# Gathering the second down product one set later, its row split moved up to the rows' multiplication

## The chip, the cores and the metric

The kernel runs on one core of one Trainium2 chip. The metric is the device time of one execution in microseconds (us); lower is better. The engines are named as the profile names them: PE (TensorE matmuls), PEld (its weight loads), DVE (VectorE), ACT (ScalarE), POOL (GpSimd) and SP (SyncE, which here only issues DMA transfers).

## What is computed

Two transformer layers over 512 tokens of width 1024: a gated mixing layer, then an attention layer with a forget gate, each followed by a feed-forward block. The change touches only the feed-forward block, which both layers run:

```python
h = h + rmsnorm(mixed @ w_out[layer], ln_mix_post[layer])
f = rmsnorm(h, ln_ffn_pre[layer])
f = (jax.nn.silu(f @ w_ffn_gate[layer]) * (f @ w_ffn_up[layer])) @ w_ffn_down[layer]
h = h + rmsnorm(f, ln_ffn_post[layer])
```

All of it is float32. `D_FF` is 2816, that is 22 blocks of 128 hidden rows.

## The kernel before

**Precision.** A float32 operand is split into two parts: `hi`, a cast to the PE's float32 format on ACT (L267), and `lo`, the rest, a subtraction on DVE (L268). `mm3` (L208 to L212) multiplies hi by hi, one hi by the other's lo, and lo by hi: three matmuls for each product of two tiles. Weights are split as `whi` and `wlo` (eight buffers each), the rows of a down product as `ff`.

**Sets.** Sixteen of the 22 hidden blocks go through a seven-product scheme in place of eight products. `Seven` (L1028) computes one *set*: two blocks of gate or of up. Its products are numbered 1 to 7 and run in the order 1, 7, 6, 4, 2, 5, 3; product 3 is run after products 1 and 7 of the next set. A product is twelve matmuls 256 wide and needs one weight split (512 wide). `form` makes the weight sums on DVE (L1055, L1056, L1059, L1061). For a gate set from j = 2 on, two sums come ready from DRAM; an up set makes all four, beginning with L1055, which reads both halves of a freshly loaded pair of weight tiles. Those tiles (`raw`) have four buffers; a new load waits until the last weight split of the tile that had the buffer is done. The loop over j = 0 to 7 (`ones` is 8) alternates a gate set and an up set; I call the two a *pair*. At the end of a set its rows come out: L1095 adds the two PSUM results and so frees their bank; `gate_rows` (L1224) multiplies by the norm and applies Silu; `up_rows` (L1230) multiplies the up rows by the gate rows: row 1 first (L1232, into `room`, called `u1`), then row 0 (L1234, into `u0`). `Down.sums` (L1110) then makes the sums that the down products need.

**Down products.** The result of pair j goes into a `Down` object, which also has seven products, here P0 to P6, each six matmuls 512 wide: three for each of two token blocks. Each needs the split of 256 columns of its rows (`ff`, six buffers of tag `p`, shared with other tiles) and a weight split. P2 accumulates over all j into one pair of PSUM banks, `kept` (tag `tr`, two buffers; the trace names the tiles `x`), while the gate and up sets go on; `straight` (L1246) loads its weights `a12`, runs it and makes `last_sum`. The other products run afterwards: a first pass over j with P0, P3, P5, P6, then a second pass with P1 and P4. I write P2(j), P5(j) and so on for those of pair j.

**Where P2 stands before.** In the loop of L1253 the condition L1272 calls `straight(j - 1, False)` after the up set for j = 1 and after the gate set for every later j. The last one, P2(7), stands in the first pass between P3(0) and P5(0); after it two ACT copies (L1306) empty `kept`, and its two banks are given to P6, which accumulates over j.

**Order.** The program's text gives a priority; a scheduler then fixes one order of instructions for each engine and of DMA issues on SP. In the trace every engine but the weight loads goes through its rows in that order, so an instruction that waits holds up those behind it. The matmul order on PE stays close to the text; DVE, ACT and SP are interleaved by the scheduler.

Of the kernel before, what the change touches and what calls it, by code (L numbers as in the profile page):

```python
# [8 lines left out]
F32R = mybir.dt.float32r  # L9
# [6 lines left out]
P = 128  # L16
# [19 lines left out]
HALVES = ((0, 256), (256, 512))  # L36
# [6 lines left out]
def hybrid(ctx: ExitStack, tc: tile.TileContext, i: dict, out: bass.AP):  # L43
# [4 lines left out]
    tp = ctx.enter_context(tc.tile_pool(name="temps", bufs=4))  # L48
# [9 lines left out]
    def name(s):  # L58
        n_of[s] = n_of.get(s, 0) + 1
        return f"{s}_{n_of[s]}"  # L60
# [4 lines left out]
    def plain(s, shape=(P, T), dt=F32):  # L65
        return yp.tile(list(shape), dt, tag="y", name=name(s))
# [4 lines left out]
    def temp(s, shape=(P, T), tag="t", bufs=4, dt=F32):  # L71
        return tp.tile(list(shape), dt, tag=tag, name=name(s), bufs=bufs)
# [12 lines left out]
    o = ps("tr", s="idle")  # L85
# [122 lines left out]
    def mm3(o, w, x, start, stop, more=False):  # L208

        PE.matmul(o, w[0], x[0], start=start, stop=False, skip_group_check=more)  # L210
        PE.matmul(o, w[0], x[1], start=False, stop=False, skip_group_check=more)  # L211
        return PE.matmul(o, w[1], x[0], start=False, stop=stop, skip_group_check=more)  # L212
# [53 lines left out]
    def split(src, hi, lo, eng=None):  # L266
        last_hi[0] = A.copy(hi, src)  # L267
        last_split[0] = last_hi[0], (eng or V).tensor_sub(lo, src, hi)  # L268
# [14 lines left out]
    class Norm:  # L283


        def __init__(self, width=T):
            self.r4 = small("r4")
            self.acc, self.width = None, width
# [739 lines left out]
    class Seven:  # L1028
# [20 lines left out]
        def form(self, n):  # L1049

            a11, a12, a21, a22 = self.a11, self.a12, self.a21, self.a22
            if n == 7:
                if not self.summed:
                    self.s3 = temp("s3")
                    V.tensor_add(self.s3, a11, a21)  # L1055
                    V.tensor_add(a21, a21, a22)  # L1056
                return self.s3
            if n == 6:
                V.tensor_add(a11, a21, a11)  # L1059
            elif n == 3:  # L1060
                V.tensor_add(a12, a11, a12)  # L1061
            return {1: a11, 2: a12, 3: a12, 4: a22, 5: a21, 6: a11}[n]

        def product(self, o, x, n, more=False):
            pair = pair_of_parts()
            split(self.form(n), *pair)
            for k, w in enumerate(cut(pair, P)):
                mm3(o, w, self.xs[x][k], k == 0 and not more, k == KT // 2 - 1, more)
# [33 lines left out]
    class Down:  # L1102
# [2 lines left out]

        def __init__(self, layer, k, u0, u1, t):
            self.layer, self.k, self.u0, self.u1, self.t = layer, k, u0, u1, t
            self.forms = {}

        def sums(self):  # L1110

# [33 lines left out]

        def product(self, n, o, start, stop):

            left, right = (slice(*c) for c in HALVES)
            if n == 3:
                V.tensor_add(self.a11, self.a21, self.a11)  # L1150
            elif n == 5:
                V.tensor_add(self.a12, self.a11, self.a12)
            src = {0: "a11", 1: "s3", 2: "a12", 3: "a11", 4: "a22", 5: "a12", 6: "a21"}[n]
            u, c = {0: (self.u0, left), 1: (self.t, left), 2: (self.u1, left), 3: (self.t, right),
                    4: (self.u1, left), 5: (self.u1, right), 6: (self.u0, right)}[n]
            both = tp.tile([P, 2, 256], F32R, tag="p", name=name("ff"), bufs=6)
            split(u[:, c], both[:, 0], both[:, 1])
            w = pair_of_parts()
            split(getattr(self, src), *(x.rearrange("p (m c) -> p m c", c=P) for x in w))
            for t in range(2):  # L1160
                tokens = slice(t * P, (t + 1) * P)
                mm3(o[t], (both[:, 0, tokens], both[:, 1, tokens]), w, start, stop, True)

    def feed_forward(layer, phase, xp, meanwhile=None):
# [3 lines left out]
        ones = 8  # L1168
# [47 lines left out]
        downs, gates = [], {}  # L1216
# [13 lines left out]
        def up_rows(row, u, some):  # L1230
            if row:
                V.scalar_tensor_tensor(out=u, in0=u, scalar=-1.0, in1=gates[1], op0=ALU.mult, op1=ALU.mult)  # L1232
            else:
                V.tensor_mul(u, u, gates[0])  # L1234
            if some:
                split(u, *some[row])
            elif not row:
                downs[-1].sums()

        def sets(m, some=None):  # L1240
            sums_ahead()
            yield Seven(xs, "w_gate", layer, m, "mm", gate_rows)
            sums_ahead()
            yield Seven(xs, "w_up", layer, m, "lg", lambda row, u: up_rows(row, u, some), None if some else places)

        def straight(j, last):  # L1246
            d = downs[j]
            d.weights(0)
            d.product(2, kept, False, last)
            d.last_sum()  # L1250

        before = lambda: None
        for j in range(ones):  # L1253
            if j == 0:
                us = list(sets(2))
                for n in (1, 2):
                    for u in us:
                        u.run(n)
                for n in (7, 6, 4, 5):
                    for u in us:  # L1260
                        u.run(n)
                us[0].run(3)
                before = us[1]
                continue
            for n, u in enumerate(sets(2 + 2 * j)):
                u.run(1)
                u.run(7)
                before.run(3)
                for x in (6, 4, 2, 5):
                    u.run(x)  # L1270
                before = u
                if n == (j == 1):  # L1272
                    straight(j - 1, False)
        before.run(3)

        o = {0: [ps("mm", s="p") for _ in range(2)], 3: [ps("lg", s="p") for _ in range(2)]}
        one, two = [act("ua", F32) for _ in range(2)], [act("ub", F32) for _ in range(2)]

        def tap(n):

            for t in range(2):
                x, y = o[n][t], ys[t]
                z = ys[2 + t]
                if n == 0:
                    A.copy(one[t], x)
                    V.tensor_add(y[0], x, y[0])
                elif n == 3:
                    V.tensor_add(one[t], x, one[t])
                elif n == 6:
                    V.tensor_add(two[t], x, one[t])  # L1290
                elif n == 5:
                    V.tensor_add(z[0], x, z[0])
                elif n == 1:
                    V.tensor_add(z[1], x, z[1])
                    V.tensor_add(y[1], x, y[1])
                else:
                    V.tensor_add(y[1], x, y[1])

        for j, d in enumerate(downs):
            d.weights(1)  # L1300
            for n in (0, 3, 5, 6) if j == 0 else (0, 3, 6, 5):
                if j == 0 and n == 5:
                    straight(ones - 1, True)
                    for t in range(2):
                        ys[t][0] = plain("y")
                        A.copy(ys[t][0], kept[t])  # L1306
                    o[5] = [ps(tag, s="p") for tag in ("mm", "lg")]
                    o[6] = [ps("tr", s="p") for _ in range(2)]
                d.product(n, o[n], j == 0, j == ones - 1)
                if j == ones - 1:  # L1310
                    tap(n)
        o.update({1: [ps("mm", s="q") for _ in range(2)], 4: [ps("lg", s="q") for _ in range(2)]})
        late = [(z, t, d) for z, d, some in ((2, 0, two), (2, 1, two), (0, 1, one)) for t in range(2)]
        for j, d in enumerate(downs):
# [5 lines left out]
            if j < len(late):  # L1320
                z, t, dh = late[j]
                y = ys[z + t][dh]
# [350 lines left out]
```

## Time and profile before

| | |
|---|---|
| median of 3 runs | 1110.28 us (1109.08 to 1110.86) |
| the profiled execution | 1109.39 us, its span 1107.7 us |
| PE busy | 1087.1 us, 98% of the span |
| PEld | 985.4 us, 89% |
| DVE | 934.4 us, 84% |
| ACT | 733.0 us, 66% |
| POOL | 59.7 us, 5% |

The profiled execution took 0.89 us less than the median. A row of the timeline gives start, duration, engine, source line, operation, `out<-in`, and in brackets how long the engine had stood idle and what ended the wait. Matmul durations overlap, since they are pipelined: what a matmul costs in a stream is the distance to the next start. The windows view gives busy time by engine in a stretch, then the granted share of the PE clock, the DMA engines' busy share and GB/s.

The loop over the pairs lies at about 200 to 378 us in the first layer and 784 to 964 us in the second.

### The profile page before, as it was taken

The numbers are of one execution on the slowest core, as the hardware profiler recorded it, in microseconds if no ns is written. First come the engines' busy times: TensorE is split into PE (matmuls) and PEld (weight loads), VectorE is DVE, ScalarE is ACT, GpSimd is POOL, SyncE is SP. The second block draws the span as 40 slices with busy tenths as digits, with TensorE's granted clock in tenths as the row PEclk, the third lists the DMA queues.
The fourth block names the chain that finished last, engine by engine and source line by source line (L and its number), as shares of the span: only waits on it lengthen the run. The fifth ranks groups of instructions, "written<-read, shape, count | busy, mean of one in ns | idle before, by whom it ended". The sixth has DMA issues, their size and how long they took to land.

```text
span 1107.7 us, 19986 instructions
## 1 busy us (share of the span) xinstructions
PE 1087.1 (98%) x7286; PEld 985.4 (89%) x7286; DVE 934.4 (84%) x1839; ACT 733.0 (66%) x1609; POOL 59.7 (5%) x74
## 2 busy tenths in 40 slices
PE   9999999999999999999999999999999999999997
PEld 7998889999999888998988898889999899888996
DVE  7889658988887999986987798858998887999975
ACT  8776468665666667677666677768666566666563
POOL 0100001001100000000000000011011010000000
PEclk9999999999999999999999999999999999999999
DMA  7522346498788445563322654445499779444622
GB/s 268 160 79 77 96 114 202 113 248 210 213 209 206 142 139 168 207 183 104 103 90 62 175 130 113 138 114 177 127 244 223 211 195 223 142 127 136 216 78 77
DMA packets 126378, 172.69 MB, mean 156 GB/s; under 512 B 7820, under 2 KB 91800, under 8 KB 126280
## 3 DMA queue, kind: packets, MB, share of 16 engines
q1 hardware_dynamic: 114920, 153.93, 45.2%
q0 software_dynamic: 10944, 17.30, 10.0%
q8 instruction: 57, 0.93, 0.3%
q14 instruction: 41, 0.34, 0.1%
q10 hardware_dynamic: 416, 0.18, 0.1%
HBM read 155.04 MB, written 39.85 MB: 176 GB/s over the span
## 4 chain that ended last, share of the span: by engine, by line
PE 79%; DVE 10%; ACT 3%; DMA 3%; issue 3%; SPq 1%; POOL 0%; DVEq 0%; POOLq 0%; ACTq 0%
PE a L210 5%; PE a L211 5%; PE a L212 5%; DVE wlo L268 5%; PE y L210 4%; PE y L211 4%; PE y L212 4%; PE ps L212 3%; PE ps L211 3%; PE ps L210 3%; PE p L212 3%; PE p L210 3%; PE p L211 3%; PE e L210 2%; PE e L211 2%
## 5 line engine op out<-in xcount | busy, mean ns | idle before, releaser
L267 ACT CAST whi<-raw 128x512 fp32r<-128x512 f32 x476 | 286.0, 619 | 122.6 <-PE a L211 21.7
L268 DVE TENSOR_TENSOR wlo<-raw,whi 128x512 fp32r<-128x512 f32 x476 | 316.7, 684 | 39.1 <-ACT whi L267 34.8
L210 PE MATMUL a<-xshi,whi 128*128 128x256 f32 x480 | 136.7, 285 | 0.0
L211 PE MATMUL a<-xslo,whi 128*128 128x256 f32 x480 | 136.2, 284 | 0.0
L212 PE MATMUL a<-xshi,wlo 128*128 128x256 f32 x480 | 135.9, 283 | 0.0
L210 PEld LDWEIGHTS a<-xshi,whi 128*128 128x128 f32 x480 | 91.8, 191 | 1.7 <-ACT e L1094 0.6
L211 PEld LDWEIGHTS a<-xslo,whi 128*128 128x128 f32 x480 | 91.9, 191 | 0.8
L212 PEld LDWEIGHTS a<-xshi,wlo 128*128 128x128 f32 x480 | 91.8, 191 | 0.0
L211 PE MATMUL ps<-xslo,whi 128*128 128x256 f32 x192 | 53.9, 283 | 0.6 <-DVE xslo L268 0.6
L212 PE MATMUL ps<-xshi,wlo 128*128 128x256 f32 x192 | 54.3, 285 | 0.0
L210 PE MATMUL ps<-xshi,whi 128*128 128x256 f32 x192 | 53.7, 287 | 0.0
L210 PE MATMUL y<-whi,mixedhi 128*128 128x512 f32 x128 | 51.6, 403 | 0.0
L211 PE MATMUL y<-wlo,mixedhi 128*128 128x512 f32 x128 | 50.6, 395 | 0.0
L210 PE MATMUL p<-whi,ff 128*128 128x512 f32 x128 | 50.5, 395 | 0.0
L212 PE MATMUL p<-whi,ff 128*128 128x512 f32 x128 | 50.5, 394 | 0.0
L212 PE MATMUL y<-whi,mixedlo 128*128 128x512 f32 x128 | 50.4, 394 | 0.0
L211 PE MATMUL p<-wlo,ff 128*128 128x512 f32 x128 | 50.4, 394 | 0.0
L869 DVE TENSOR_TENSOR y<-y,y 128x512 f32<-128x512 f32 (+1 forms) x33 | 22.2, 673 | 30.4 <-PE y L212 30.3
L210 PE MATMUL e<-t,whi 128*128 128x256 f32 x160 | 45.0, 281 | 0.0
L210 PE MATMUL e<-t3hi,whi 128*128 128x256 f32 x160 | 45.0, 281 | 0.0
L210 PE MATMUL x<-xshi,whi 128*128 128x256 f32 x160 | 45.0, 281 | 0.0
L211 PE MATMUL x<-xslo,whi 128*128 128x256 f32 x160 | 45.0, 281 | 0.0
(356 smaller groups left out, 3493.5 us busy)
## 6 DMA issues: line engine op xcount, KB each, us to landing
raw<-in_w_up SPq DMA_DIRECT2D x44, 512.0 KB, 4.1
raw<-in_w_gate SPq DMA_DIRECT2D x28, 512.0 KB, 4.5
raw<-in_w_down SPq DMA_DIRECT2D x28, 512.0 KB, 4.4
raw<-in_w_out SPq DMA_DIRECT2D x16, 512.0 KB, 4.1
sums<-in_w_gate SPq DMA_DIRECT2D x16, 512.0 KB, 5.8
sums<-in_w_gate POOLq DMA_DIRECT2D x16, 512.0 KB, 6.3
sums<-in_w_down SPq DMA_DIRECT2D x32, 256.0 KB, 6.8
sums<-in_w_down POOLq DMA_DIRECT2D x16, 512.0 KB, 6.9
```

The costliest lines, as they stand in the source:

```text
L210: PE.matmul(o, w[0], x[0], start=start, stop=False, skip_group_check=more)
L211: PE.matmul(o, w[0], x[1], start=False, stop=False, skip_group_check=more)
L212: return PE.matmul(o, w[1], x[0], start=False, stop=stop, skip_group_check=more)
L267: last_hi[0] = A.copy(hi, src)
L268: last_split[0] = last_hi[0], (eng or V).tensor_sub(lo, src, hi)
L869: (V.tensor_sub if turned_sign and dh else V.tensor_add)(y, o[:, cols], y)
```

## The change

Four things change, all in `Down` and `feed_forward`.

1. `straight(j - 1, False)` is called after the up set for every j, so P2(j - 1) for j = 2 to 7 stands one set later.
2. The split of P2's rows becomes `Down.form(2)` and is called in `up_rows` directly behind the multiplication of row 1. Its buffers are those of tag `acc` (two) in place of `p`. Other products still split their rows where they multiply.
3. The first pass begins with P0, P3, P5 of pair 0 and the same of pair 1; only then P2(7), the two copies of `kept`, P6(0) and P6(1). From pair 2 on it is P0, P3, P6, P5 as before. P5's banks are allotted ahead of the pass.
4. The weights of P2(7) are loaded ahead of the first pass.

```diff
+        def form(self, n):
+
+            left, right = (slice(*c) for c in HALVES)
+            u, c = {0: (self.u0, left), 1: (self.t, left), 2: (self.u1, left), 3: (self.t, right),
+                    4: (self.u1, left), 5: (self.u1, right), 6: (self.u0, right)}[n]
+            tag, bufs = ("acc", 2) if n == 2 else ("p", 6)
+            both = self.parts[n] = tp.tile([P, 2, 256], F32R, tag=tag, name=name("ff"), bufs=bufs)
+            split(u[:, c], both[:, 0], both[:, 1])
...
         def product(self, n, o, start, stop):
...
-            both = tp.tile([P, 2, 256], F32R, tag="p", name=name("ff"), bufs=6)
-            split(u[:, c], both[:, 0], both[:, 1])
+            if n not in self.parts:
+                self.form(n)
+            both = self.parts.pop(n)
...
             if row:
                 V.scalar_tensor_tensor(out=u, in0=u, scalar=-1.0, in1=gates[1], op0=ALU.mult, op1=ALU.mult)
+                if not some:
+                    downs[-1].form(2)
...
         def straight(j, last):
             d = downs[j]
-            d.weights(0)
+            if not last:
+                d.weights(0)
...
-                if n == (j == 1):
+                if n:
                     straight(j - 1, False)
...
-        for j, d in enumerate(downs):
-            d.weights(1)
-            for n in (0, 3, 5, 6) if j == 0 else (0, 3, 6, 5):
-                if j == 0 and n == 5:
-                    straight(ones - 1, True)
-                    for t in range(2):
-                        ys[t][0] = plain("y")
-                        A.copy(ys[t][0], kept[t])
-                    o[5] = [ps(tag, s="p") for tag in ("mm", "lg")]
-                    o[6] = [ps("tr", s="p") for _ in range(2)]
-                d.product(n, o[n], j == 0, j == ones - 1)
+        def first_pass(j, some):
+            if 0 in some:
+                downs[j].weights(1)
+            for n in some:
+                downs[j].product(n, o[n], j == 0, j == ones - 1)
                 if j == ones - 1:
                     tap(n)
+
+        o[5] = [ps(tag, s="p") for tag in ("mm", "lg")]
+        downs[-1].weights(0)
+        for j in range(2):
+            first_pass(j, (0, 3, 5))
+        straight(ones - 1, True)
+        for t in range(2):
+            ys[t][0] = plain("y")
+            A.copy(ys[t][0], kept[t])
+        o[6] = [ps("tr", s="p") for _ in range(2)]
+        for j in range(2):
+            first_pass(j, (6,))
+        for j in range(2, ones):
+            first_pass(j, (0, 3, 6, 5))
```

Two places on the engines show what the scheduler makes of it. The first is DVE in the middle of the loop of the first layer, before the change, around the split for P2(4) (`ff_4107`); `wlo_4193`, `wlo_4211` and `wlo_4227` are the splits for products 6, 4 and 2 of the up set that follows P2 on PE:

```order
L1234 TENSOR_TENSOR u_3850<-u_3850,s_5_3696 128x512
L1114 TENSOR_TENSOR t_3851<-room_2516,u_3850 128x256
L268 TENSOR_TENSOR wlo_4193<-raw_4124,whi_4192 128x512
L1115 TENSOR_TENSOR u_3850<-u_3850 128x256
L1116 SCALAR_TENSOR_TENSOR t_3851<-u_3850,room_2516 128x256
L268 TENSOR_TENSOR wlo_4211<-raw_4126,whi_4210 128x512
L268 TENSOR_TENSOR wlo_4227<-raw_4124,whi_4226 128x512
L268 TENSOR_TENSOR ff_4107<-room_2516,ff_4107 128x256
```

And in the changed kernel, the same pair from the first sum of its up set's weights (L1055) to the same split (now `ff_4032`):

```order
L1055 TENSOR_TENSOR s_8_4139<-raw_4111,raw_4113 128x512
L268 TENSOR_TENSOR wlo_4074<-raw_3970,whi_4073 128x512
L1056 TENSOR_TENSOR raw_4113<-raw_4113 128x512
L268 TENSOR_TENSOR wlo_4091<-raw_3968,whi_4090 128x512
L1095 TENSOR_TENSOR room_2516<-e_3839,room_2516 128x512
L1061 TENSOR_TENSOR raw_3970<-raw_3970 128x512
L1239 SCALAR_TENSOR_TENSOR room_2516<-room_2516,s_5_3697 128x512
L268 TENSOR_TENSOR wlo_4117<-raw_4111,whi_4116 128x512
L268 TENSOR_TENSOR wlo_4138<-s_8_4139,whi_4137 128x512
L268 TENSOR_TENSOR ff_4032<-room_2516,ff_4032 128x256
```

The split has moved from the eighteenth place behind its pair's L1055 to the ninth, and L1055 now stands ahead of the split for product 2 of the gate set (`wlo_4074`), behind which it stood before: from one L1055 to the split that frees the raw tiles there are 28 operations where there were 27.

The second place is ACT at the beginning of the first pass in the first layer. Before, the two copies that empty `kept` (`y_4934`, `y_4936`) stand in the middle of the casts for pair 1:

```order
L267 CAST ff_4973<-u_2943 128x256
L267 CAST whi_5017<-raw_4969 128x512
L267 CAST ff_4987<-t_2944 128x256
L1306 COPY y_4934<-x_2448 128x512
L267 CAST ff_5000<-u_2943 128x256
L1306 COPY y_4936<-x_2449 128x512
L267 CAST ff_5014<-room_2516 128x256
L267 CAST whi_5034<-raw_5027 128x512
```

In the changed kernel they (`y_4995`, `y_4997`) stand behind the weight casts of pair 2 for P0, P3, P6 and P5 (`whi_5034`, `whi_5048`, `whi_5061`, `whi_5075`):

```order
L267 CAST whi_5034<-raw_5027 128x512
L267 CAST ff_5031<-u_3243 128x256
L267 CAST ff_5045<-t_3244 128x256
L267 CAST ff_5058<-u_3243 128x256
L267 CAST whi_5048<-raw_5027 128x512
L267 CAST whi_5061<-t_5028 128x512
L267 CAST whi_5075<-raw_5027 128x512
L267 CAST ff_5072<-room_2516 128x256
L1324 COPY y_4995<-x_2448 128x512
L267 CAST whi_5092<-raw_5085 128x512
L1324 COPY y_4997<-x_2449 128x512
```

`whi_5048` and `whi_5075` read weight tiles after sums that DVE makes in place (L1158 and L1160 in the changed kernel, L1150 and L1152 before), so the copies now stand behind those two sums of pair 2 as well.

More of the change, by code (lines that the diff above doesn't have):

```diff
@@ L1107, in __init__ @@
             self.layer, self.k, self.u0, self.u1, self.t = layer, k, u0, u1, t
-            self.forms = {}
+            self.parts = {}
+        def form(self, n):
[5 more added lines that the diff above has]
+            split(u[:, c], both[:, 0], both[:, 1])
         def sums(self):
@@ L1146, in product @@
         def product(self, n, o, start, stop):
-            left, right = (slice(*c) for c in HALVES)
             if n == 3:
@@ L1153, in product @@
             src = {0: "a11", 1: "s3", 2: "a12", 3: "a11", 4: "a22", 5: "a12", 6: "a21"}[n]
-            u, c = {0: (self.u0, left), 1: (self.t, left), 2: (self.u1, left), 3: (self.t, right),
-                    4: (self.u1, left), 5: (self.u1, right), 6: (self.u0, right)}[n]
-            both = tp.tile([P, 2, 256], F32R, tag="p", name=name("ff"), bufs=6)
-            split(u[:, c], both[:, 0], both[:, 1])
+            if n not in self.parts:
+                self.form(n)
+            both = self.parts.pop(n)
             w = pair_of_parts()
```

## The prediction

> **What bounds the kernel now.** I read the page's busy shares, then who waits on PE, then the timeline around one such wait, then DVE and SP in the same stretch.
>
> ```profile
> span 1107.7 us, 19986 instructions
> PE 1087.1 (98%) x7286; PEld 985.4 (89%) x7286; DVE 934.4 (84%) x1839; ACT 733.0 (66%) x1609; POOL 59.7 (5%) x74
> PE x L212 <- DVE ff L268: 9.4, 10, 1.9
> 242.00 0.40 PE L210 MATMUL x<-whi,ff 128*128 128x512 f32 x1
> 242.24 0.40 PE L211 MATMUL x<-wlo,ff 128*128 128x512 f32 x1
> 242.48 0.39 PE L212 MATMUL x<-whi,ff 128*128 128x512 f32 x1
> 253.74 0.39 PE L211 MATMUL x<-wlo,ff 128*128 128x512 f32 x1
> 255.99 0.50 PE L212 MATMUL x<-whi,ff 128*128 128x512 f32 x1 [1.85 <-DVE ff L268]
> 884.19 0.50 PE L212 MATMUL x<-whi,ff 128*128 128x512 f32 x1 [1.85 <-DVE ff L268]
> 257.20:260.60 3.40, 3.40 (x18) 3.40 (x18) 2.55 (x5) 1.75 (x4) 0.84 (x1) 0.50 0.57 161
> 885.30:888.70 3.40, 3.40 (x18) 3.40 (x17) 2.42 (x5) 1.52 (x4) 0.85 (x1) 0.50 0.37 104
> ```
>
> PE is busy nearly throughout, and its one large wait is the one that the change is about: P2's third matmul waits for the `ff` split, 9.4 us over ten waits. P2(0), at 242, runs without a stop: starts lie 0.24 apart, so a P2 is six times 0.23, 1.4 us. P2(1) has 2.25 between two starts, a stop of 2.0 us; 1.2 us after it PE gets half its clock for 3.4 us, and the same follows the stop that ends at 884.19 in the second layer: 1.7 us lost each time.
>
> Is PE then held by the place of the split alone, or by something that would hold it elsewhere? One pair in the steady state:
>
> ```profile
> 312.00 0.69 DVE L1055 TENSOR_TENSOR s<-raw,raw 128x512 f32<-128x512 f32 x1 [1.61 <-DMA raw<-in_w_up]
> 315.02 0.68 DVE L1095 TENSOR_TENSOR room<-e,room 128x512 f32<-128x512 f32 x1
> 315.62 0.68 DVE L268 TENSOR_TENSOR wlo<-raw,whi 128x512 fp32r<-128x512 f32 x1
> 322.29 0.42 DVE L268 TENSOR_TENSOR ff<-room,ff 128x256 fp32r<-128x256 f32 x1
> 322.76 0.50 PE L212 MATMUL x<-whi,ff 128*128 128x512 f32 x1 [0.28 <-DVE ff L268]
> 323.80 0.28 PE L210 MATMUL a<-xshi,whi 128*128 128x256 f32 x1
> 327.98 0.69 DVE L268 TENSOR_TENSOR wlo<-raw,whi 128x512 fp32r<-128x512 f32 x1 [0.68 <-ACT whi L267]
> 328.70 0.33 SPq L140 DMA_DIRECT2D raw<-in_w_up  x1
> 334.43 0.69 DVE L1055 TENSOR_TENSOR s<-raw,raw 128x512 f32<-128x512 f32 x1 [2.09 <-DMA raw<-in_w_up]
> 343.67 0.46 PE L210 MATMUL x<-whi,ff 128*128 128x512 f32 x1
> 246.90:356.75 109.85, 106.73 (x847) 103.62 (x846) 91.26 (x158) 67.69 (x147) 10.96 (x10) 0.98 0.86 217
> 829.60:941.75 112.15, 107.92 (x863) 105.03 (x862) 91.46 (x158) 67.89 (x149) 11.02 (x10) 0.98 0.85 214
> ```
>
> Two things are to be seen. The weight splits run far ahead: the one at 315.62 is for the product that PE begins at 323.80. Only `ff` comes just in time, since it stands behind the splits of later products. But there is a **loop without PE**: L1055 waits for a load, and 16.67 us after its start (312.00 to 328.67) the split ends that frees the buffer for the next load, which SP issues at 328.70 and which lands at 334.43, 5.76 us later. 16.67 + 5.76 = 22.43, the whole pair. PE itself needs fourteen products, 19.9 us (from the first, at 323.80, to the next P2 at 343.67), and a P2: 19.9 + 1.4 = 21.3 us. The five rounds between the first and last L1055 of these loops took 109.85 us in the first layer and 112.15 in the second, 22.0 and 22.4 each. So P2's stop is where PE pays for being faster than a loop of DVE and DMA.
>
> **The change part by part.** I call the last L1055 of a loop U (356.75 and 941.75).
>
> *The stop at P2* goes: its split stands nine places earlier on DVE, and P2 itself comes a set, some 10 us, later. PE then runs at 21.3 a pair.
>
> *The loop of DVE and DMA.* The order has 28 operations in place of 27 between L1055 and the freeing split, +0.60 (315.02 to 315.62 is such a step). The 0.68 wait in the row at 327.98 goes; it is DVE waiting for ACT, which waits for buffers that PE has not released, and PE will now be early. Balance −0.08 a round: the loop stays at 22, and PE lives on DVE's lead, losing 0.6 to 1.1 us of it a pair. What does shorten are the rounds in which PE's stop and half clock had held DVE up:
>
> ```profile
> 260.12 0.69 DVE L268 TENSOR_TENSOR wlo<-raw,whi 128x512 fp32r<-128x512 f32 x1 [0.85 <-ACT whi L267]
> 262.71 0.69 DVE L268 TENSOR_TENSOR wlo<-raw,whi 128x512 fp32r<-128x512 f32 x1 [1.29 <-ACT whi L267]
> 843.88 0.69 DVE L268 TENSOR_TENSOR wlo<-raw,whi 128x512 fp32r<-128x512 f32 x1 [0.48 <-ACT whi L267]
> 888.45 0.69 DVE L268 TENSOR_TENSOR wlo<-raw,whi 128x512 fp32r<-128x512 f32 x1 [0.98 <-ACT whi L267]
> 890.91 1.52 DVE L268 TENSOR_TENSOR wlo<-raw,whi 128x512 fp32r<-128x512 f32 x2 [1.16 <-ACT whi L267]
> 895.77 0.69 DVE L1055 TENSOR_TENSOR s<-raw,raw 128x512 f32<-128x512 f32 x1 [0.52 <-DMA raw<-in_w_up]
> ```
>
> First layer: 0.85 + 1.29, and four times 0.08: U comes 2.4 us earlier. Second: 0.5 at 844 and 2.1 − 0.6 = 1.5 at 888 to 891, with the small rest 2.5. Here I take off 0.4: the split at 890.91 ended at 891.60, and the load behind it landed 4.2 later, not 5.8, so a late release was partly made up. U 2.1 earlier; bounds 0 (landing times set by the DMA engines, 0.85 busy) and 2.5.
>
> *The first pass* is where the lead is missed.
>
> ```profile
> 356.75 0.69 DVE L1055 TENSOR_TENSOR s<-raw,raw 128x512 f32<-128x512 f32 x1 [2.00 <-DMA raw<-in_w_up]
> 376.32 0.69 DVE L268 TENSOR_TENSOR wlo<-t,whi 128x512 fp32r<-128x512 f32 x1 [0.33 <-ACT whi L267]
> 377.75 0.69 DVE L268 TENSOR_TENSOR wlo<-raw,whi 128x512 fp32r<-128x512 f32 x1 [0.73 <-ACT whi L267]
> 379.08 0.68 DVE L1095 TENSOR_TENSOR room<-e,room 128x512 f32<-128x512 f32 x1
> 383.70 0.59 ACT L1306 COPY y<-x 128x512 f32<-128x512 f32 x1
> 384.49 0.59 ACT L1306 COPY y<-x 128x512 f32<-128x512 f32 x1
> 389.37 0.69 DVE L1152 TENSOR_TENSOR raw<-raw 128x512 f32<-128x512 f32 x1
> 392.57 0.40 PE L210 MATMUL p<-whi,ff 128*128 128x512 f32 x1
> 977.59 0.40 PE L210 MATMUL p<-whi,ff 128*128 128x512 f32 x1
> ```
>
> P6(0) needs the banks of `kept`, so the copies, which ACT now reaches only after casting pair 2's P5 weights, which needs L1160 on DVE. That sum stood at U + 32.6 before (389.37). In the new order there are as many operations up to it, one half-width (0.34) replaced by a full one (0.60); the two waits on ACT (1.06) go, since they were DVE at its largest lead. So U + 31.8, done at U + 32.5; then the cast of P5's weights, an `ff` cast of half the width and the copy, 0.59 at 383.70 and by their widths 0.6 and 0.3 for the casts: U + 34 to 34.5, I take 34.3. PE is there earlier. Its last hold before that is P5(0), whose second bank is freed by L1095: 22.3 after U before (379.08), now two full and two half operations more, minus the waits: U + 23.1, done 23.8. Behind it half of P5(0), then P0(1), P3(1), P5(1) and P2(7), 6.3 us: U + 30.1 to 30.5. So **PE stops about 4 us at P6(0)**. Behind PE there wait P6, the rest of P0(2) and the whole pass. P0(2) goes on 2.8 − 0.2 after P6(0): U + 36.9, against 35.8 before in both layers (392.57 − 356.75, 977.59 − 941.75): +1.05 each. The price lies between 0 (copies soon enough) and 2.1 (the two waits stay).
>
> *The clock.* A stop of 2.0 us in one stretch was followed by 3.4 us at half clock, twice, while the next shorter one, 1.5 us, was not:
>
> ```profile
> 950.75 0.40 PE L211 MATMUL x<-wlo,ff 128*128 128x512 f32 x1
> 952.50 0.50 PE L212 MATMUL x<-whi,ff 128*128 128x512 f32 x1 [1.36 <-DVE ff L268]
> ```
>
> Both low stretches are 3.4 long, and I take the clock to be decided in steps of that length. A stop of 4 us always puts 2 us or more into one step; the next one is then at half clock, part of it perhaps inside the stop, or two are: 0.8 to 2.4 lost, I take 1.5 for each layer. [...]
>
> *At no cost:* the `acc` buffers (two; a split is used within about 20 us of its writing, a pair takes 21), the earlier load of P2(7)'s weights, and the swap of `a12` and `a22` on SP, behind the freeing split's load as before. What covers them is DVE's lead, 8 us (315.62 against 323.80) at first and, after five pairs that cost 0.6 to 1.1 each, 3 to 5 at the end; without it each late split would stop PE by its delay.
>
> **Sum.** First layer −2.4 + 1.05 + 1.5 = +0.15; second −2.1 + 1.05 + 1.5 = +0.45; together +0.6 on the profiled 1109.39 us (span 1107.7 and 1.7 around it): 1110.0. That execution was 0.9 below the median of 1110.28, so 1110.9 in medians: **no change**.
>
> **Rivals.**
>
> *B, the copies are not late.* If DVE is 4 us further ahead in the first pass than I count, P6(0) runs at U + 30.5 and no clock is lost: 3.8 + 1.5 less for each layer, 10.6 together: 1100.3. For it: before, DVE kept its full lead through the loop. Against: L1055 waits for the load every time, 2.0 us even at 356.75.
>
> *C, nothing else binds.* All stops at P2 go and none comes: 9.4 by the row, some 11 by starts, and 3.4 of clock: 1096. For it: PE's 98% and the lead of 8 us. Against: a round takes 22.0 and 22.4 against PE's 21.3. [...]
>
> *D, slower: the DMA engines set the landing times.* Then the loop doesn't shorten at all where DVE releases earlier, U stays, and the first pass and the clock cost 2 × 2.55 = 5.1: 1115.4. It decides once the load takes 0.5 us longer a round. For it: 0.86 and 0.85 DMA busy, and the short load at 895.77 after a late release. Against: the 109.85 us of the first layer, where equal weights landed sooner.
>
> *E, the change does nothing on PE.* The order shows P2 moved; only if its wait merely changes place one for one, 1110.
>
> **How the numbers follow.** About 0.2% (2.2 us) is what a measurement of this kernel can tell from no change. My forecast (about 1111, its own range 1108 to 1114): 0.50, of which 0.03 falls below 1108.1 and 0.14 above 1112.5. B 0.14, C 0.10, D 0.22, E 0.04. Faster 0.14 + 0.10 + 0.03 = 0.27; same 0.33 + 0.04 = 0.37; slower 0.22 + 0.14 = 0.36. The range takes in B and D and leaves out C and D's worst (two low steps in a layer): 1099 to 1116.
>
> **What would show it.** Right: no wait of `x L212` for `ff`; L1055 still waiting for DMA in every pair, the five rounds at 107 to 110 us; a wait of PE at a P6 matmul for the ACT copy of 3 to 4.5 us, at about U + 30, with half clock behind it. Wrong: no such wait (B), L1055 without DMA waits (C), or five rounds of 110 us and more with PE waiting on `wlo` inside the loop (D, or worse).

## The result and the profile after

The changed kernel takes 1112.52 us (median of 12 runs, 1107.13 to 1114.48), the kernel before, on the same chip, 1111.73 us (12 runs, 1107.52 to 1113.28). The ratio is 1.0003, its 95% interval 0.9987 to 1.0019: no change that can be told. The forecast was no change, 1110.9 us. Where the time went inside is another matter, and the forecast had that only in part.

The profiled execution of the changed kernel took 1112.7 us. From its page, the span and the busy line; then the waits of PE, of DVE and of ACT that matter here (engine, line, what was waited for: us in total, times, longest):

```profile
span 1111.0 us, 19990 instructions
PE 1086.8 (98%) x7286; PEld 984.2 (89%) x7286; DVE 936.6 (84%) x1839; ACT 729.6 (66%) x1609; POOL 59.6 (5%) x74
PE e L210 <- ACT s L1083: 5.7, 7, 1.4
PE e L210 <- ACT room L1083: 5.1, 8, 1.3
PE a L210 <- ACT e L1094: 2.0, 2, 1.0
DVE s L1055 <- DMA raw<-in_w_up: 25.9, 11, 3.4
ACT ff L267 <- DVE room L1239: 27.0, 12, 2.7
```

P2 no longer waits for `ff` at all. In its place PE waits at **product 4** of a set (`e`), for an ACT copy, L1083, that has to read the result of product 7 out of the same bank before product 4 may go on in it: 5.7 us in gate sets and 5.1 in up sets; and 2.0 us at product 3 of the last up set. That is 12.8 us. Before, PE lost 9.4 at P2 and two times 1.7 to the half clock behind it, also 12.8. In sum the wait has changed its place.

The five rounds between the first and last L1055 of each loop, in the windows view (us; then busy time and count of PE, PEld, DVE, ACT, POOL; clock, DMA share, GB/s):

```profile
247.09:357.87 110.78, 107.95 (x870) 105.05 (x869) 90.78 (x156) 67.19 (x150) 10.96 (x10) 1.00 0.86 217
833.95:942.49 108.54, 107.31 (x869) 104.71 (x868) 90.78 (x157) 67.01 (x150) 11.02 (x10) 1.00 0.87 221
```

22.2 and 21.7 a round, where it was 22.0 and 22.4. The clock is 1.00 in both: neither loop has half clock now. One such stop, in the timeline of DVE, ACT and PE:

```profile
289.85 0.69 DVE L1055 TENSOR_TENSOR s<-raw,raw 128x512 f32<-128x512 f32 x1 [2.87 <-DMA raw<-in_w_up]
292.26 0.68 DVE L1095 TENSOR_TENSOR room<-e,room 128x512 f32<-128x512 f32 x1
293.46 0.68 DVE L1239 SCALAR_TENSOR_TENSOR room<-room,s 128x512 f32<-128x512 f32 x1
294.23 0.41 ACT L267 CAST ff<-room 128x256 fp32r<-128x256 f32 x1 [2.71 <-DVE room L1239]
294.55 0.61 ACT L267 CAST whi<-raw 128x512 fp32r<-128x512 f32 x1
295.07 0.36 ACT L1083 COPY s<-e 128x256 f32<-128x256 f32 x1
294.28 0.28 PE L212 MATMUL a<-d2hi,wlo 128*128 128x256 f32 x1
295.48 0.39 PE L210 MATMUL e<-t,whi 128*128 128x256 f32 x1 [0.92 <-ACT s L1083]
```

Read it from the top. DVE waits 2.87 us for the up weights. Six places behind L1055 stands L1239, the multiplication of the up rows; the cast of `ff`, which the change brought forward, waits for it and holds ACT for 2.71 us. Behind that cast stand a weight cast and the copy L1083, and PE goes on 0.41 us after that copy began. So at this place PE is tied to the landing of the up weights, 5.63 us behind L1055, as P2 was before, by another way. It is the way of the gate sets; the up sets' stops come by others. In the last up set of each layer it is the Silu (L1234) that stands ahead of the copy and waits 2.50 us for L1233 on DVE, and in pair 1 a weight cast that waits for a gate load:

```profile
238.05 0.62 ACT L267 CAST whi<-raw 128x512 fp32r<-128x512 f32 x1 [2.34 <-DMA raw<-in_w_gate]
373.24 0.63 ACT L1234 ACTIVATE s<-s 128x512 f32<-128x512 f32 x1 [2.50 <-DVE s L1233]
```

That later instructions of ACT wait behind one that waits is seen in the three rows of ACT above: the last matmul of product 7 starts at 292.05 and takes 0.28, but the copy that reads its result starts at 295.07, 0.84 us behind the cast that waited until 294.23.

The loop itself, a round later:

```profile
311.69 0.69 DVE L1055 TENSOR_TENSOR s<-raw,raw 128x512 f32<-128x512 f32 x1 [1.93 <-DMA raw<-in_w_up]
324.19 5.01 SPq L140 DMA_DIRECT2D raw<-in_w_up  x2
327.36 1.48 DVE L268 TENSOR_TENSOR wlo<-raw,whi 128x512 fp32r<-128x512 f32 x2
334.70 0.69 DVE L1055 TENSOR_TENSOR s<-raw,raw 128x512 f32<-128x512 f32 x1 [3.09 <-DMA raw<-in_w_up]
```

The freeing split is the second of the two at 327.36; it ends at 328.84, 17.15 after L1055, and the load behind it lands 5.86 later: 23.01, the round.

### The profile page after: what moved, and what is told of

It is laid out like the page before. It is cut to its first block, busy times and chain, and to the rows that moved or that the text cites. A ratio compares the mean times of both kernels' runs of the same rounds, so it can differ in the third digit from the quotient of the medians.

```text
span 1111.0 us, 19990 instructions
## 1 busy us (share of the span) xinstructions
PE 1086.8 (98%) x7286; PEld 984.2 (89%) x7286; DVE 936.6 (84%) x1839; ACT 729.6 (66%) x1609; POOL 59.6 (5%) x74
## 4 chain that ended last, share of the span: by engine, by line
PE 71%; DVE 12%; DMA 6%; ACT 6%; issue 4%; POOL 0%; SPq 0%; DVEq 0%; POOLq 0%; ACTq 0%
DVE wlo L268 5%; PE y L210 4%; PE y L211 4%; PE y L212 4%; DMA raw<-in_w_up 3%; PE a L210 3%; PE a L211 3%; PE a L212 3%; PE ps L212 3%; PE ps L211 3%; PE ps L210 3%; PE p L210 3%; PE p L212 3%; PE p L211 3%; ACT whi L267 2%
## 5 line engine op out<-in xcount | busy, mean ns | idle before, releaser
L212 PE MATMUL a<-xshi,wlo 128*128 128x256 f32 x480 | 134.5, 280 | 0.0
L212 PEld LDWEIGHTS a<-xshi,wlo 128*128 128x128 f32 x480 | 90.4, 188 | 0.0
L210 PE MATMUL e<-t,whi 128*128 128x256 f32 x160 | 47.2, 295 | 11.1 <-ACT s L1083 5.7
L212 PE MATMUL ps<-xshi,wlo 128*128 128x256 f32 x192 | 54.3, 285 | 0.0
L212 PE MATMUL y<-whi,mixedlo 128*128 128x512 f32 x128 | 50.4, 394 | 0.0
L212 PE MATMUL p<-whi,ff 128*128 128x512 f32 x128 | 50.2, 394 | 0.0
L869 DVE TENSOR_TENSOR y<-y,y 128x512 f32<-128x512 f32 (+1 forms) x33 | 22.2, 673 | 30.4 <-PE y L212 30.3
L211 PE MATMUL e<-t,whi 128*128 128x256 f32 x160 | 45.0, 281 | 0.0
```

The lines of the kernel that those rows point to most:

```text
L869: (V.tensor_sub if turned_sign and dh else V.tensor_add)(y, o[:, cols], y)
```

## The experiments

Three theories stood against each other. *Loop*: L1055, the freeing split and the load behind it set the round, whatever holds PE. *Queue*: ACT's order alone made the new stops. *First pass*: the loop gained and the new first pass gave it back. The kernel before was run beside each group: 1111.54, 1111.63 and 1112.11 us.

### Parts of the change

**late_gather_only** leaves out the early split:

```diff
                 V.scalar_tensor_tensor(out=u, in0=u, scalar=-1.0, in1=gates[1], op0=ALU.mult, op1=ALU.mult)
-                if not some:
-                    downs[-1].form(2)
```

> Only parts 1, 3 and 4 of the change: P2 one set later, its row split left where the product is (the call in up_rows taken out). Loop theory (DVE and the load set the round of about 22 us, PE at 21.3 must stop somewhere): the scheduler puts the cast and the split of these rows at nearly the same places anyway, so the same as the changed kernel, 1110 to 1115 us, with PE waiting some 10 to 14 us at product 4 for the ACT copy L1083. Split theory (the early place of the split is what took away the stop at P2): P2's third matmul waits for ff again, 5 us or more, and some half clock with it: 1114 to 1120 us.

1110.36 us, ratio 0.9987 (0.9969 to 1.0005). The view of waits:

```profile
PE e L210 <- ACT s L1083: 7.7, 9, 2.1
DVE s L1055 <- DMA raw<-in_w_up: 31.0, 12, 4.1
```

PE waits at product 4 in this kernel too: with another 1.6 us in up sets that is 9.3 us, a little under the 10 to 14 expected. P2 doesn't wait for `ff`. The scheduler had put the cast of `ff` between the same two rows of ACT and its split one place later on DVE; once P2 itself stands a set later, the second part of the change is hardly a change.

**early_split_only** has only that part: the split early, P2 in its old place (the diff is against the changed kernel) and the first pass in its old order, as in old_first_pass below.

```diff
-                if n:
+                if n == (j == 1):
                     straight(j - 1, False)
```

> Part 2 of the change alone: the split of P2's rows directly behind their multiplication, P2 and the first pass in their old places. On DVE the split then stands directly behind the multiplication, as in the changed kernel. Loop theory: P2's waits for ff go, and the stops come at product 4 behind L1083 as in the changed kernel: 1109 to 1114 us. If the later P2 was needed to remove the wait: x L212 still waits 4 us or more, 1110 to 1114 us. The PE waits tell the two apart, not the time.

1111.83 us, ratio 1.001 (0.9995 to 1.0025). P2's waits for `ff` are gone here as well, and the whole price stands at product 4:

```profile
PE e L210 <- ACT s L1083: 10.7, 10, 2.1
PE e L210 <- ACT room L1083: 1.6, 2, 1.2
```

12.3 us. Either part alone moves the stop from P2 to product 4; neither removes it.

**old_first_pass** has the loop of the changed kernel and the old order behind it:

```diff
+        for j in range(ones):
+            for n in (0, 3, 5, 6) if j == 0 else (0, 3, 6, 5):
+                if j == 0 and n == 5:
+                    straight(ones - 1, True)
...
+                first_pass(j, (n,))
-        for j in range(2):
-            first_pass(j, (0, 3, 5))
-        straight(ones - 1, True)
...
-        for j in range(2, ones):
-            first_pass(j, (0, 3, 6, 5))
```

> Parts 1, 2 and 4 in the loop, but the first pass as before: P2(7) and the copies of kept between P3(0) and P5(0). Loop theory: what PE lost in the changed kernel it lost in the loop, at product 4; the first pass gave nothing back, so 1111 to 1114 us, and the five rounds between the L1055s take 108 to 111 us as in the changed kernel. First-pass theory (the loop gained 5 us and the new first pass took them back): 1106 to 1108 us.

1110.23 us, ratio 0.9986 (0.9971 to 1.0001): between the two expectations, 2.3 us below the changed kernel's median, with intervals that overlap. The waits at product 4 are 5.8 and 4.2 us. The gain of 5 us that the first-pass theory needs is not there; that the new order costs some 2 us in this loop is possible, and the intervals don't settle it.

### ACT's queue

**copy_ahead** puts the copy L1083 ahead of three casts that wait for DVE:

```diff
-            split(self.form(n), *pair)
+            w = self.form(n)
+            end = self.seven if n == 3 else last_seven[0] if n == 7 else None
+            with behind(*([end] if end else [])):
+                split(w, *pair)
...
-                A.copy(self.s2[:, right], self.q[:, left])
+                self.seven = last_seven[0] = A.copy(self.s2[:, right], self.q[:, left])
...
-            split(u[:, c], both[:, 0], both[:, 1])
+            with behind(*([last_seven[0]] if n == 2 else [])):
+                split(u[:, c], both[:, 0], both[:, 1])
```

> The changed kernel with three of ACT's casts (the ff rows of P2, the weights of product 3 and those of the next product 7) held behind the copy L1083 of the set on PE, so that this copy no longer stands behind a cast that waits for DVE. Loop theory: the waits at a gate set's product 4 (5.7 us in the changed kernel) go to under 1.5 us, but the rounds stay (five of them 108 to 111 us), and PE stops instead at an up set's product 4, at a weight split or at P6(0): 1109 to 1114 us. Queue theory (ACT's order alone made the new stops): they go and nothing comes, 5 to 6 us less than the changed kernel, 1104 to 1107 us.

1117.21 us, ratio 1.005 (1.003 to 1.0069), slower than either theory said. The gate sets' wait is gone, and the five rounds took 106.9 and 111.2 us, where 108 to 111 were expected. The loss lies in the first two pairs of each layer: from the second L1055 to the first of the five rounds it takes 4.3 us longer in each than in the changed kernel. There the sets run in another order; that the edit holds casts which PE needs soon would explain it, and wasn't followed. **copy_ahead_late** applies the same edit from the third pair on (`steady[0] = j > 1`, and `and steady[0]` in both conditions).

> copy_ahead lost about 6 us in the first two pairs of each layer, before the steady loop, where its order makes L1055 come 29.1 us after the first one instead of 23.1. Here the same three casts are held behind L1083 only from the third pair on; DVE's order stays that of the changed kernel. Loop theory: the last five rounds of each layer still take 108 to 112 us, the waits at a gate set's product 4 for L1083 are gone, others of PE take their place, and the time is that of the changed kernel, 1109 to 1115 us. Queue theory: PE's waits for ACT in the loop fall by the 5.7 us and nothing takes their place: 1104 to 1107 us.

1111.2 us, ratio 0.9993 (0.9975 to 1.0011). PE's waits in the loop and behind it, and the windows. The edit shifts the lines: L1088 is the copy L1083 of the changed kernel, L1083 the copy of product 1 (L1078), L1091 that of product 6, L1099 that of product 5, L1332 the copy of `kept`:

```profile
PE e L212 <- ACT room L1088: 4.5, 6, 1.8
PE a L212 <- ACT s L1091: 3.1, 4, 1.1
PE a L212 <- ACT x L1083: 1.0, 1, 1.0
PE a L212 <- ACT e L1099: 0.8, 2, 0.4
PE p L212 <- ACT y L1332: 0.8, 2, 0.4
246.88:357.16 110.28, 108.83 (x883) 106.51 (x882) 90.37 (x158) 67.68 (x152) 10.96 (x10) 1.00 0.86 215
830.54:941.35 110.81, 108.63 (x874) 105.69 (x873) 89.95 (x156) 66.92 (x151) 11.02 (x10) 1.00 0.85 216
```

The gate sets' wait for the copy L1083 (5.7 us) is gone, and the rounds stay at 22.1 and 22.2. PE still stops at product 4 of the up sets, and now also for the copies of products 6, 1 and 5, and a little at P6(0): 10.2 us in these rows. The queue decides where PE stops; it does not decide how long the round is.

### The loop

**sum_behind_rows** holds L1055 on DVE behind the multiplication of the up rows (`last_row`), and nothing else:

```diff
-                    V.tensor_add(self.s3, a11, a21)
+                    with behind(*([last_row[0]] if last_row[0] else [])):
+                        V.tensor_add(self.s3, a11, a21)
...
-                V.scalar_tensor_tensor(out=u, in0=u, scalar=-1.0, in1=gates[1], op0=ALU.mult, op1=ALU.mult)
+                last_row[0] = V.scalar_tensor_tensor(out=u, in0=u, scalar=-1.0, in1=gates[1], op0=ALU.mult, op1=ALU.mult)
```

> The changed kernel with L1055 held on DVE behind the multiplication of the up rows (L1239 of the profile's kernel before this edit). From L1055 to the split that frees the raw tile there are then 21 operations in place of 28, 7 x 0.60 = 4.2 us less, and DVE has work to do while the load is under way. Loop theory: 22.4 - 4.2 = 18.2 us is below PE's 21.3, so the rounds fall to 21.2 to 21.8 (five of them 106 to 109 us), L1055 waits for the load much less, the stops at product 4 of the gate sets go: 1098 to 1104 us. Queue theory: only the gate sets' 5.7 us go, 1106 to 1107. If the DMA engines set the landing times (rival D), rounds stay at 21.8 to 22.4 and the time at 1109 to 1113 us.

1095.37 us, ratio 0.9856 (0.983 to 0.9881): 16 us less than the kernel before, and some 3 us below the expectation of the loop theory. DVE's timeline over a round, and the two windows (L1057 and L1241 are L1055 and L1239):

```profile
307.74 0.69 DVE L1241 SCALAR_TENSOR_TENSOR room<-room,s 128x512 f32<-128x512 f32 x1
308.96 0.43 DVE L269 TENSOR_TENSOR ff<-room,ff 128x256 fp32r<-128x256 f32 x1
309.30 0.69 DVE L1057 TENSOR_TENSOR s<-raw,raw 128x512 f32<-128x512 f32 x1
321.10 1.51 DVE L269 TENSOR_TENSOR wlo<-raw,whi 128x512 fp32r<-128x512 f32 x2
330.50 0.68 DVE L1057 TENSOR_TENSOR s<-raw,raw 128x512 f32<-128x512 f32 x1
246.71:351.78 105.07, 105.07 (x862) 103.77 (x861) 95.20 (x160) 69.60 (x150) 10.98 (x10) 1.00 0.87 223
822.77:927.83 105.06, 105.06 (x864) 103.72 (x863) 95.25 (x161) 69.77 (x150) 11.03 (x10) 1.00 0.88 226
```

The weight sum stands without a wait. From it to the end of the freeing split are 13.31 us (309.30 to 322.61), 3.8 less than 17.15, and 7.9 us are left for a load. The round is 21.2 us (309.30 to 330.50): PE's own 21.3 as the prediction had worked it out, and PE is busy in the whole of both windows. Of the 15.9 us between the two profiled executions 11.9 lie in the ten rounds; 4.5 lie behind the last L1055 of the two loops, where PE no longer stops either; the expectation named only the rounds and the gate sets' stops. The DMA engines, at 0.87 and 0.88, carry more GB/s than before (223 and 226 against 217 and 214), so they had not set the pace. The edit does two things: it takes seven operations out of the loop, and it takes the multiplication of the rows out from behind a wait for a load. No run parts the two, but only the first shortens the way from one L1055 to the next, which made up the whole round before.

**five_raw** was to open the same loop with a fifth buffer, at the price of one `whi` and one `wlo`:

```diff
-        return wp.tile([P, 1024], F32, tag="raw", name=name("raw"), bufs=4)
+        return wp.tile([P, 1024], F32, tag="raw", name=name("raw"), bufs=5)
...
-        return tuple(wp.tile([P, 2 * WIDE], F32R, tag=t, name=name("w" + t), bufs=8)[:, :n] for t in ("hi", "lo"))
+        return tuple(wp.tile([P, 2 * WIDE], F32R, tag=t, name=name("w" + t), bufs=7)[:, :n] for t in ("hi", "lo"))
```

> The changed kernel with five buffers of raw tiles in place of four, and, to make room, seven each of whi and wlo in place of eight. A load is then issued one tile earlier, about half a set or 5 us. Loop theory: the loop no longer closes within a round, L1055 hardly waits for its load, rounds of 21.2 to 21.8 us (five: 106 to 109), 1096 to 1104 us; as much as sum_behind_rows or some us less of it, since DVE can run one split less ahead. If the load's own time on the DMA engines set the pace, it would be no better than 1109 us.

1124.78 us, ratio 1.0129 (1.0102 to 1.0156): the expectation was wrong. A round of it:

```profile
338.74 0.69 DVE L1055 TENSOR_TENSOR s<-raw,raw 128x512 f32<-128x512 f32 x1 [2.32 <-DMA raw<-in_w_up]
349.77 5.93 SPq L140 DMA_DIRECT2D raw<-in_w_up  x2
354.64 0.69 DVE L268 TENSOR_TENSOR wlo<-raw,whi 128x512 fp32r<-128x512 f32 x1
361.39 0.69 DVE L1055 TENSOR_TENSOR s<-raw,raw 128x512 f32<-128x512 f32 x1 [2.68 <-DMA raw<-in_w_up]
```

The second up load is issued at the end of its row, just behind the split that ends at 355.33, 16.6 after L1055, and lands 6.1 later: the same loop. A pair has four raw tiles. With five buffers the second up tile takes the buffer of the first up tile of the pair before, and that is the one that the freeing split reads; L1055 needs both tiles. By the same count six buffers would part them; that wasn't tried. The five rounds took 110.57 and 110.91 us, so the 13 us lost lie outside them: from the last L1055 of the first layer to the first of the second layer it takes 328.5 us instead of 315.4. (The first layer's second L1055 comes 9.2 us later, but 8.2 of them are made up by its last.) PE also ran five stretches of 3.41 us at half clock, where the changed kernel had none before its last microseconds (from 1106.3 us on): the clock over the profiled execution was 0.991 here and 0.998 there; two of them, 1.7 us each at most, lie between the layers. Only the count of buffers was changed; which of the splits outside lacks them wasn't followed.

### What the change is worth once the loop is open

**sum_behind_rows_old** is the kernel before with the edit of sum_behind_rows and nothing of the change. To tell it from sum_behind_rows both were run once more as **behind_old_again** and **behind_again**, beside **behind_early_split** (early_split_only with that edit) and **behind_old_pass** (old_first_pass with it).

> The kernel before (P2 in its old place, its split with the product) with L1055 held behind the rows' multiplication as in sum_behind_rows. Loop theory: the loop is shortened here too, and then the old place of P2 sets what PE waits for: the split of ff still stands 14 places behind the multiplication on DVE, so that some of the 9.4 us of waits and the half clock behind them stay: 1098 to 1106 us, 3 to 10 us above sum_behind_rows (1095.4). If the later P2 is worth nothing even then: 1094 to 1097 us.

> sum_behind_rows once more, beside the three below, since 2.4 us between it and sum_behind_rows_old are no more than their intervals: 1094 to 1097 us. Loop theory: with the loop out of the way what is left of the change's effect shows by itself, so this one should be the fastest or equal.

> sum_behind_rows_old once more. If the stop at P2 is worth what its rounds showed (21.42 against 21.25 us, and about 1 us in the round of P2(1)), 1.5 to 3 us above behind_again: 1096 to 1099 us. If the difference was chance: within 1 us of it.

> early_split_only with L1055 held behind the rows' multiplication: P2 and the first pass in their old places, its split early. If the early split is all that counts once the loop is out of the way: within 1 us of behind_again, rounds of 21.2 to 21.3 us and no wait of x L213 for ff. If the later place of P2 is needed: as behind_old_again or slower, 1096 to 1099 us.

> sum_behind_rows with the first pass in its old order. If the new order of the first pass costs or saves nothing: within 1 us of behind_again. If the copies of kept behind pair 2's casts hold up PE by the 1 us that the prediction's step put on each layer, 2 us below it.

| L1055 behind the rows, and | us | ratio to the kernel before, 95% interval |
|---|---|---|
| nothing else (sum_behind_rows_old) | 1097.79 | 0.9883 (0.9863 to 0.9902) |
| the same again (behind_old_again) | 1098.39 | 0.9883 (0.986 to 0.9905) |
| early split alone (behind_early_split) | 1095.13 | 0.9854 (0.9831 to 0.9876) |
| all but the new first pass (behind_old_pass) | 1094.72 | 0.985 (0.9828 to 0.9872) |
| the whole change (sum_behind_rows) | 1095.37 | 0.9856 (0.983 to 0.9881) |
| the same again (behind_again) | 1095.95 | 0.9858 (0.9836 to 0.9879) |

The one edit gives about 14 us without anything of the change, 1097.79 where 1098 to 1106 or 1094 to 1097 were expected. What the change, or any part that takes P2's split forward, then saves besides is some 2.5 us; it came out twice alike, though the intervals overlap. behind_early_split, with no wait of P2 and rounds of 21.2 to 21.3 from the second on, shows that the early split is enough for it. In sum_behind_rows_old the trace has:

```profile
PE x L213 <- DVE ff L269: 1.4, 2, 1.1
246.47:354.35 107.88, 107.58 (x874) 105.12 (x873) 95.07 (x161) 68.97 (x150) 10.97 (x10) 1.00 0.86 221
```

The same wait at P2, now 1.4 us, and five rounds of 107.88 instead of 105.07. Most of that last difference is not loss: PE ran 874 matmuls in the one window and 862 in the other. The four rounds behind the first are 21.4 us each against 21.2 to 21.3. The new order of the first pass is worth nothing that can be told: 1094.72 with the old one, 1095.95 with the new one in the same group, 1.2 us apart, between the two expectations.

## Why the prediction was right, and where it was not

**Right: the loop.** The core of the forecast was that P2's stop was only the place where PE pays for being faster than a loop of DVE and DMA, and that the change leaves that loop alone. L1055 still waits for its load, eleven times (twelve before), the time stays, and opening the loop gave 16 us while PE ran at 21.2 us a round, where the prediction had counted 21.3 for it.

**Right: the stop at P2 goes.** No wait of `x L212` is left.

**Off: the size of the loop.** Its 28th operation was to cost 0.60 and a wait of 0.68 to go: 16.6. It measured 17.15. The operation came, the wait went from its place, but DVE now meets several of 0.1 to 0.2 us along the way. From the first L1055 (its second tile, 203.46 and 203.97) to U the first layer took 153.29 before and 153.90 after, +0.6, where −2.4 was forecast; the second 154.69 and 151.95, −2.7 for −2.1. Loads of 4.3 to 6.1 us in single rounds make up such differences; one profiled execution of each kernel does not settle them. The sum had slipped here, too: by its own balance the added 0.60 belongs into every round, also into that of the 0.85 and 1.29 and that of the wait at 844; then U comes 1.9 us earlier in the first layer and 1.7 in the second before the 0.4, and the forecast 1.3 us higher, still no change. The five rounds were to take 107 to 110 us: 110.78 and 108.54.

**Wrong: "PE lives on DVE's lead".** That step counted the lead in weight splits, 8 us, and let PE use it up until the first pass. The shortest lead was not there but on ACT: in gate sets the copy L1083 stood behind the cast of `ff`, which waited for L1239, which stood six places behind L1055. On that way PE had next to no lead, and it stopped there in seven of the twelve gate sets from pair 2 on, 0.27 to 1.39 us each. In an up set of pair 1 (239.51, 1.09 us) it had already stopped behind the cast that waited for a gate load. copy_ahead_late shows both halves of this: with another order on ACT the gate sets' stops go, and the rounds stay.

**Wrong in place, near in size by luck: the first pass.** These are rows of the first layer behind U (357.87):

```profile
363.51 0.39 PE L210 MATMUL e<-t,whi 128*128 128x256 f32 x1 [1.27 <-ACT s L1083]
374.71 0.39 PE L210 MATMUL e<-t,whi 128*128 128x256 f32 x1 [1.00 <-ACT room L1083]
381.61 0.39 PE L210 MATMUL a<-xshi,whi 128*128 128x256 f32 x1 [1.00 <-ACT e L1094]
390.68 0.69 DVE L1160 TENSOR_TENSOR raw<-raw 128x512 f32<-128x512 f32 x1
392.56 0.57 ACT L1324 COPY y<-x 128x512 f32<-128x512 f32 x1
393.18 0.19 PEld L210 LDWEIGHTS p<-whi,ff 128*128 128x128 f32 x1 [0.32 <-ACT y L1324]
```

The sum L1160 of pair 2 starts at U + 32.8, where 31.8 was worked out, and the first copy of `kept` ends at U + 35.3 (392.56 and 0.57), where 34.3 was: the step was right in kind and 1.0 us short. But PE had already stood three times, comes to P6(0) only some 0.3 us before that copy ends, not 4 us, and waits no more than that. By the sign that the prediction had set for itself, a wait of 3 to 4.5 us there, this step failed; B, which that sign would speak for, did not come true either: its P6(0) was to run at U + 30.5. P0(2) is at U + 38.0 in both layers, 2.1 later than before: the upper bound of the term, not its 1.05.

**The clock** was to cost 1.5 more in each layer; none of the three stops was followed by half clock, and that term is zero.

From U to that L1055 of the second layer (790.54) it takes 432.7 us, 2.4 more than before; from the second U to the end of the span 168.5, 2.6 more. That each comes close to the 2.55 that were forecast is luck: three stops inside the last sets and a later copy stand in place of one stop at P6(0) and a low clock. In old_first_pass, where the third of the three stops is missing, the same two stretches take 1.0 us more than before each, so some 1.5 of them come with the new order in these traces. And with a loop that gained 2.1 us in both layers together in place of 4.5, the whole came out near the forecast by terms that were each off: +0.8 us in the medians and +3.3 between the profiled executions, for the +0.6 forecast.

**The rivals.** B and C asked for a free PE, and it was not free. D, that the DMA engines set the landing times, falls with sum_behind_rows, which moved 223 and 226 GB/s in those windows, where 217 and 214 were moved before. E, that the wait merely changes place one for one, was given 0.04 and named no place; in sum it is what the rows of the result show, 12.8 us for 12.8, though not place by place: 6.6 of the new 12.8 are the three stops behind U in both layers, where P2 had cost 2.1 before.

## What to carry to other kernels

When the engine that sets the time waits for another one, look for the closed loop behind the wait: from the instruction that waits for a load to the one that frees the buffer, and back. If that loop is longer than the engine's own work, moving the wait only moves it. To shorten it, put work that is ready ahead of the instruction that waits for the load, and count a lead on every queue that releases something, the small copies out of PSUM too, since the shortest one decides. Before adding a buffer, count which tile's buffer each load takes: in five_raw the load that L1055 waits for still took the one that is freed last, and the loop stayed.

## What the runs showed of the hardware

Which stop is followed by half clock is not told by its length alone. In copy_ahead_late a wait of 1.77 us was followed by a stretch of 3.41 us at half clock, and in late_gather_only one of 2.12 us; in five_raw one of 2.12 us, just as long, was not. The rows of PE and the windows behind them, in this order:

```profile
239.05 0.38 PE L212 MATMUL e<-t,whi 128*128 128x256 f32 x1 [1.77 <-ACT room L1088]
240.46:243.87 3.41, 3.41 (x19) 3.41 (x18) 3.33 (x6) 2.99 (x6) 0.03 (x1) 0.50 0.70 115
```

```profile
904.87 0.38 PE L210 MATMUL e<-t,whi 128*128 128x256 f32 x1 [2.12 <-ACT s L1083]
906.12:909.53 3.41, 3.41 (x18) 3.41 (x17) 3.34 (x8) 1.79 (x5) 0.00 (x0) 0.50 0.92 247
```

```profile
912.76 0.39 PE L210 MATMUL a<-xshi,whi 128*128 128x256 f32 x1 [2.12 <-ACT room L1086]
912.80:916.20 3.40, 3.40 (x23) 3.13 (x24) 3.25 (x6) 2.51 (x6) 0.27 (x1) 1.00 0.73 119
```

The prediction took the clock to be decided in steps of 3.4 us, and the traces agree with that. In the kernel before, three stretches at half clock begin at 257.22, 885.27 and 1103.72 us; the first two are 3.413 us long, and the distances are 184 and 64 times 3.413 us, to within 0.1. The five stretches at half clock in five_raw begin at 37.71, 191.31, 297.13, 556.54 and 785.23 us: the distances are 45, 31, 76 and 67 times 3.413 us, to within 0.1. Counted on from there, the stop of 2.12 us in five_raw (910.64 to 912.76) lies across the end of a step, at 911.5; that of late_gather_only (902.75 to 904.87) lies inside the step of 3.41 us that ends where the half clock begins, at 906.12, and so does that of copy_ahead_late (237.28 to 239.05, half clock from 240.46). So in these three the half clock followed the stops that lay inside one step. That it matters how much of a stop falls into one step is an estimate from them; no run was made to test it.

The kernel before spreads over 1106.43 to 1115.87 us in 24 runs of one group, and sum_behind_rows over 1093.45 to 1096.33 in four. With the loop open the landing time of each load no longer enters the round, which would explain it; the few runs don't show it.
